# Moving a two-layer decoder kernel's operands by 96 bytes, reading its position bias reversed, and spreading the down products over the last quad

## The chip, the cores and the metric

The kernel runs on one core of a Trainium2 chip, as one program in one launch. The metric is device time in microseconds (us). Before the change three runs took 2271.83, 2272.42 and 2274.74 us, so the median is 2272.42 us. Smaller is better.

## The reference

Two layers of a decoder trunk work on 512 positions of 1024 channels, in float32. Each layer is

```
x = x + 0.5 * SwiGLU(RMSNorm(x))          # FFN 1, hidden width 2816
h = RMSNorm(x);  z = h @ w_in             # one combined projection
p_A = conv module, p_B = short gated conv
p_C = sliding-window attention (window 128, shared T5 relative bias)
p_D = forgetting attention
x = x + (sum_i sigmoid(gate_i) * p_i) @ w_out
x = x + 0.5 * SwiGLU(RMSNorm(x))          # FFN 2
```

The relative bias that p_C adds to its scores depends only on the distance between query and key. For one head it is a band matrix: row p is one fixed line of 384 numbers, shifted by p places. The kernel builds that matrix once, as the tile `bias` (128 partitions, 4 heads, 256 keys), and uses it in both layers.

## The kernel before, in words

**Arithmetic.** Every large product is done as three matmuls in the type float32r: each operand is split into a high part and a rest, and `mm3` sums high x high, high x rest and rest x high. The stationary operand is 128x128, and each matmul loads its own. Moving operands are 512 columns wide in the projections and the down products (`X` and `hs` tiles, and `L` tiles in the mixer), and 256 wide in most of the FFN (`th` high, `tl` rest).

**Weights.** They stream from HBM in chunks of 512 KB over the SyncE (SP) queue into the tiles `ws` and `X`. ScalarE (ACT) then casts a chunk to its high part `h` (line 292) and VectorE (DVE) subtracts to get the rest `l` (line 299). `nextw` keeps a few chunks ahead of TensorE (PE).

**The FFN.** There are 22 hidden tiles. The first four are plain products against `X` (`proj`, `proj2`). Beside them DVE and ACT prepare `th` and `tl` from x, a quarter in each call of `halves`. The other 18 go in nine pairs, one per call of `quad`, by a Strassen scheme: seven products of 24 matmuls each, named by their moving operand (B11, B21, T2, T3, T1, B22, T4). In a call, `begin` issues the next pair's B11 between T1 and B22, and the last product, T4, has a chain behind it: DVE subtracts, ACT takes the Silu, DVE multiplies, ACT and DVE split the result into two `hs` tiles. The hidden tiles are cut into three segments (`SEGS`). After each segment `down` multiplies its `hs` tiles by the down weights: two groups `mg` of four 128-row outputs, and in each a loop over chunks `kc`, where chunk kc uses the hs tiles of pair kc of that segment.

**Setup.** `setup` is a generator that starts in the first FFN of the first layer and is carried on at `tick`. It makes the line of 384 numbers for each head (a matmul at line 599, an add at line 601), writes it to a scratch tensor `toep` in DRAM 128 times, row after row with a pitch of 385 (line 604), and reads `toep` back with a pitch of 384, so that row p comes out shifted by p (line 606). Both transfers are issued by GpSimd (POOL). TensorE takes no part in it beyond line 599.

**Where tiles lie.** Tiles come from pools that are laid out one behind the other in SBUF. Pool `odd` (small tiles) comes first, then `sb` (weights, x, X), then the pools of a stage. So the sum of the small tiles sets where everything behind them starts. In the program before, the weight tiles and the tiles X, L, hs, `pth` and `ptl` start 96 bytes past a multiple of 128 bytes. `th` and `tl` start 32 bytes past one, since a tile `off` of 64 bytes is put ahead of them. PSUM has two groups of four banks, `mm` and `bg`.

**Order.** The program's order on each engine is fixed when it is built: a scheduler places instructions by their dependences, so it may pull some of a later product's matmuls into a place where an engine would wait.

Of the kernel before, what the change touches and what calls it, by code (L numbers as in the profile page):

```python
# [32 lines left out]
P = 128  # L33
# [4 lines left out]
FF = 2816  # L38
NF = 22
SEGS = ((0, 8), (8, 16), (16, 22))  # L40
NSTD = 4

B11, B21, B22, T1, T3, T2, T4 = range(0, 1792, 256)
# [21 lines left out]
C_1 = 640  # L65
C_OH = 641
C_NEG = C_OH + 384
NCST = C_NEG + 384

SWA_PAIRS = ((0, 2), (1, 3))  # L70
NMM = 4
# [8 lines left out]
def _trunk(tc, xin, wst, wa, wv, wf, par, relb, cst, out):  # L80
    nc = tc.nc
    ctx = ExitStack()

    odd = ctx.enter_context(tc.tile_pool(name="odd", bufs=1))
    sb = ctx.enter_context(tc.tile_pool(name="sb", bufs=1))
    psp = ctx.enter_context(tc.tile_pool(name="ps", bufs=1, space=bass.MemoryType.PSUM))
    uid = [0]
# [17 lines left out]
    def PSM():  # L105
        uid[0] += 1
        return psp.tile([P, S], F32, tag="mm", bufs=NMM, name=f"mm_{uid[0]}")
# [84 lines left out]
    def item(kind, n, srcs, q=False, raw=RW, a1=None, turn=0):  # L192
        items.append((kind, n, srcs, raw, q, a1 or (4 if q else 2), 3 if q else 2, turn))

    def chunk(kind="w", k=1, **kw):
        nonlocal ci
        item(kind, 1024, [wst[ci + i] for i in range(k)], **kw)
        ci += k

    def ffn_items():  # L200
        for _ in range(2 * NSTD):
            chunk()
        f0, nq, q = len(items), (NF - NSTD) // 2, 0
        both = RW + RX
        chunk("A11", q=True)
        for t0, t1 in SEGS:
            for t in range(max(t0, NSTD), t1, 2):
                kw = dict(q=True, raw=both, turn=f0)
                if q:
                    chunk("A12", **kw)  # L210
                else:
                    chunk("A12", q=True)
                chunk("S2", 2, a1=None if q else 2, **kw)
                item("S3", 1024, [], **kw)
                item("S1", 1024, [], **kw)
                q += 1
                if q < nq:
                    chunk("A11", **kw)
                item("S4", 1024, [], **kw)
                item("A22", 1024, [], **kw)  # L220
            for _ in range(2 * ((t1 - t0) // 2)):
                if t1 < NF:
                    chunk(**kw)
                else:
                    chunk()
# [215 lines left out]
    def down(hs, mg, nk, after):  # L441

        pss = [PSM() for _ in range(4)]
        for kc in range(nk):
            w = kt(nextw(), S)
            for c in range(4):
                for kk in range(2):
                    mm3(pss[c], (w[0][:, kk, c * P:(c + 1) * P], w[1][:, kk, c * P:(c + 1) * P]),
                        hs[2 * kc + kk], kc == 0 and kk == 0, kc == nk - 1 and kk == 1)
                if kc == nk - 1:  # L450
                    after(4 * mg + c, pss[c])

    def ffn(st, nxt, fin=None, first=False):
        cx = open_stage("ffn", "tf")
# [56 lines left out]
            V.tensor_mul(us, us, sg)  # L511
            put(us)

        def quad(t):

            a, c11 = nxtq[0] or begin()
            w, b = nextw(), PSM()
            product(b, w, B21, True)
            V.tensor_add(c11, c11, b)
            w = nextw()  # L520
            product(a, w, T2)
            cc = T([P, 2 * S], F32, "cc", 2, pool="ffn").rearrange("p (s h c) -> p s h c", s=2, h=2)
            A.copy(cc[:, :, 0, :], gu(a))
            w, c = nextw(), PSM()
            product(c, w, T3, True)
            w = nextw()
            product(a, w, T1)
            A.copy(cc[:, :, 1, :], gu(a))
            V.tensor_sub(cc[:, :, 1, :], gu(c), cc[:, :, 1, :])
            nxtq[0] = begin() if t + 2 < NF else None  # L530
            w = nextw()
            product(a, w, B22)
            sg = TP()
            A.activation(sg[:, 0:256], c11[:, 0:256], AF.Silu)
            A.activation(sg[:, 256:S], a[:, 0:256], AF.Silu)
            V.tensor_mul(sg[:, 0:256], sg[:, 0:256], c11[:, 256:S])
            V.tensor_mul(sg[:, 256:S], sg[:, 256:S], a[:, 256:S])
            put(sg)
            w = nextw()
            product(c, w, T4)  # L540
            V.tensor_sub(cc[:, :, 0, :], gu(c), cc[:, :, 0, :])
            sg = TP()
            A.activation(sg, cc[:, 0].rearrange("p h c -> p (h c)"), AF.Silu)
            V.tensor_mul(sg, sg, cc[:, 1].rearrange("p h c -> p (h c)"))
            put(sg)

        for t0, t1 in SEGS:
            hs.clear()
            for t in range(t0, min(NSTD, t1)):
                wg, wu = kt(nextw()), kt(nextw())  # L550
                pg, pu = PSM(), PSM()
                if t < 1:
                    proj2(st, wg, pg, wu, pu)
                else:
                    halves(t)
                    proj(st, wg, pg)
                    proj(st, wu, pu)
                if first and t == 0:
                    spawn(setup())
                if t == 0:  # L560
                    halves(0)
                hidden(pg, pu, st.rb)
                tick()
            for t in range(max(NSTD, t0), t1, 2):
                quad(t)
                tick()
            last = t1 == NF

            def after(d, ps):
                stt(x[d], ps, 0.5, x[d], ALU.mult, ALU.add)  # L570
                if last and nxt is not None:
                    norm_split(nxt, d)
                if last and fin is not None:
                    fin(d)

            for mg in range(2):
                down(hs, mg, (t1 - t0) // 2, after)
            if last and nxt is not None:
                spawn(norm_end(nxt))
        cx.close()  # L580
# [6 lines left out]
    def setup():  # L587
        V.tensor_copy(idb, ident)
        V.tensor_copy(cmb, ct[:, C_CM:C_CM + P])
        rt = T([32, 4], F32, "rt")  # L590
        nc.gpsimd.dma_start(rt, relb)
        oh = TP()
        nc.gpsimd.dma_start(oh[0:32, 0:384], cst[0:32, C_OH:C_OH + 384])
        ng = TP()
        nc.gpsimd.dma_start(ng[0:4, 0:384], cst[0:4, C_NEG:C_NEG + 384])
        yield
        yield
        ps = PSB()
        mm(ps[0:4, 0:384], lhsT=rt, rhs=oh[0:32, 0:384], start=True, stop=True)
        br = TP()  # L600
        V.tensor_add(br[0:4, 0:384], ps[0:4, 0:384], ng[0:4, 0:384])
        scr = tc.dram_tile([4, P * 385], F32, name="toep")
        dst = bass.AP(tensor=scr.tensor, offset=scr.offset, ap=[[P * 385, 4], [385, P], [1, 384]])
        nc.gpsimd.dma_start(dst, br[0:4, 0:384].rearrange("p (o c) -> p o c", o=1).to_broadcast([4, P, 384]))
        src = bass.AP(tensor=scr.tensor, offset=scr.offset + 127, ap=[[384, P], [P * 385, 4], [1, 256]])
        nc.gpsimd.dma_start(bias, src)


    def mixer(l, st, nxt):
        cx = open_stage("mix", "modd")  # L610


        cacc = [None, None]
# [108 lines left out]
        def fox_unit(h, i):  # L722
# [14 lines left out]
                A.activation(p[:, 0:W], p[:, 0:W], AF.Identity, scale=sm)  # L737
                yield
                if i == 0:
                    ptile["h"] = T([P, 2048], F32R, "pth", pool="mix").rearrange("p (q j c) -> p q j c", q=4, j=4)  # L740
                    ptile["l"] = T([P, 2048], F32R, "ptl", pool="mix").rearrange("p (q j c) -> p q j c", q=4, j=4)
                    V.memset(f(ptile["h"][:, 2, 3, :]), 0.0)
                    V.memset(f(ptile["l"][:, 2, 3, :]), 0.0)
                pT = PSB()
# [28 lines left out]
        def swa_unit(pr, n):  # L773
# [23 lines left out]
                yield  # L797
                yield
                if n == 0:
                    stile["h"] = T([P, 2048], F32R, "pth", pool="mix").rearrange("p (h s c) -> p h s c", h=2, s=8)  # L800
                    stile["l"] = T([P, 2048], F32R, "ptl", pool="mix").rearrange("p (h s c) -> p h s c", h=2, s=8)
                    V.memset(f(stile["h"][:, :, 6, :]), 0.0)
                    V.memset(f(stile["l"][:, :, 6, :]), 0.0)
                pT = PSB()
# [189 lines left out]
            norm_split(nxt, d)  # L994

        for mg in range(2):
            down(mT, mg, 4, after)
        spawn(norm_end(nxt))
        cx.close()

# [30 lines left out]
def _constants():  # L1031
    c = np.zeros((P, NCST), np.float32)
    p = np.arange(P)
    c[:, C_ONE:C_ONE + P] = 1.0 / D
    c[:, C_ID:C_ID + P] = np.eye(P)
    c[:, C_TRI:C_TRI + P] = p[:, None] <= p[None]
    c[:, C_TRI + P:C_TRI + 2 * P] = 1.0
    c[:, C_CM:C_CM + P] = np.where(p[None] <= p[:, None], 0.0, NEG)
    c[:, C_1] = 1.0
    b = _buckets()  # L1040
    for e in range(384):
        dist = 255 - e
        if 0 <= dist < P:
            c[b[dist], C_OH + e] = 1.0
        else:
            c[:, C_NEG + e] = NEG
    return c
# [100 lines left out]
```

## Time and profile before

| what | value |
|---|---|
| median of three runs | 2272.42 us |
| the profiled execution's own time | 2276.64 us |
| its span (first to last instruction) | 2274.9 us |
| mean granted TensorE clock | 0.99 |
| PE busy | 2234.0 us, 98% of the span, 13059 matmuls |
| PE weight loads busy | 1973.6 us, 87% |
| DVE busy | 1542.3 us, 68% |
| ACT busy | 1004.0 us, 44% |
| POOL busy | 3.8 us |
| DMA | 217.81 MB, mean 96 GB/s |

The profile is of one execution. A busy PE means that some matmul is in its pipeline; it does not say how fast matmuls follow each other, which is read from their start times. The profile also gives the granted clock: 1.0 is the level of 2.4 GHz and 0.5 is that of 1.2 GHz. The profile divides the span into 40 slices of 57 us; the clock stands at 9 tenths or more in all of them but the second, where it stands at 6.

### The profile page before, as it was taken

The page shows a single profiled execution, that of the slowest core. Times are in us where ns is not written, and L with a number is a line of the kernel's source. Part 1 is how long each engine was busy: PE and PEld are TensorE (multiplying, and loading weights), DVE is VectorE, ACT ScalarE, POOL GpSimd, SP SyncE. Part 2 cuts the span into 40 slices and gives each one's busy share as a digit, 9 for nine tenths or more (in the row PEclk, how much of TensorE's full clock was granted, in tenths as well). Part 3 has the DMA queues.
Part 4 walks back from the last instruction along what each step waited for, and adds up shares of the span by engine and source line. Part 5 has one row for each costly group of instructions (what it writes and reads, how often), then busy time and mean ns, then how long its engine had stood idle before and what let it go on. Part 6 is the DMA issues. An engine that isn't in the chain of part 4 may idle for free.

```text
span 2274.9 us, 31903 instructions
## 1 busy us (share of the span) xinstructions
PE 2234.0 (98%) x13059; PEld 1973.6 (87%) x13059; DVE 1542.3 (68%) x2234; ACT 1004.0 (44%) x1506; POOL 3.8 (0%) x9
## 2 busy tenths in 40 slices
PE   9599999999999999999999999999999999999999
PEld 6589998988888889898989898988888888899998
DVE  7658576776665487575688585676767645957664
ACT  4335343465433355352455252454544333534432
POOL 0000000000000000000000000000000000000000
PEclk9699999999999999999999999999999999999999
DMA  5433312322223334232124232223222222432312
GB/s 147 126 112 95 119 47 84 93 81 78 75 74 100 105 95 149 90 111 94 59 90 158 95 100 93 70 86 96 75 80 69 92 93 93 130 130 85 129 47 84
DMA packets 62146, 217.81 MB, mean 96 GB/s; under 512 B 7408, under 2 KB 7540, under 8 KB 62000
## 3 DMA queue, kind: packets, MB, share of 16 engines
q1 hardware_dynamic: 61056, 214.41, 29.0%
q0 software_dynamic: 944, 1.37, 0.4%
q8 instruction: 102, 1.67, 0.3%
q14 instruction: 44, 0.36, 0.1%
HBM read 212.87 MB, written 2.88 MB: 95 GB/s over the span
## 4 chain that ended last, share of the span: by engine, by line
PE 95%; DMA 2%; DVE 1%; ACT 1%; issue 0%; SPq 0%; ACTq 0%; DVEq 0%
PE mm L347 20%; PE mm L349 20%; PE mm L348 20%; PE bg L483 6%; PE bg L486 6%; PE bg L485 6%; PE mm L483 4%; PE mm L486 4%; PE mm L485 4%; DMA ws<-wst 1%; DMA X<-wst 1%; PE bg L746 0%; PE bg L906 0%; PE bg L730 0%; PE bg L371 0%
## 5 line engine op out<-in xcount | busy, mean ns | idle before, releaser
L299 DVE TENSOR_TENSOR l<-ws,h 128x1024 fp32r<-128x1024 f32 (+2 forms) x246 | 295.9, 1204 | 345.8 <-ACT h L292 276.6
L292 ACT CAST h<-X 128x1024 fp32r<-128x1024 f32 x264 | 277.3, 1053 | 442.3 <-PE mm L348 193.1
L299 DVE TENSOR_TENSOR l<-X,h 128x1024 fp32r<-128x1024 f32 x264 | 320.7, 1221 | 186.0 <-PE mm L349 74.3
L292 ACT CAST h<-ws 128x1024 fp32r<-128x1024 f32 (+2 forms) x246 | 255.0, 1038 | 429.8 <-PE mm L348 256.3
L347 PE MATMUL mm<-X,h 128*128 128x512 f32 x928 | 364.2, 395 | 0.6 <-ACT h L352 0.5
L349 PE MATMUL mm<-X,l 128*128 128x512 f32 x928 | 363.0, 391 | 0.0
L348 PE MATMUL mm<-X,h 128*128 128x512 f32 x928 | 361.8, 391 | 0.7 <-DVE X L159 0.6
L483 PE MATMUL bg<-th,h 128*128 128x256 f32 x1152 | 327.1, 284 | 30.9 <-ACT h L292 22.2
L486 PE MATMUL bg<-th,l 128*128 128x256 f32 x1152 | 325.4, 283 | 0.6 <-DVE l L299 0.6
L485 PE MATMUL bg<-tl,h 128*128 128x256 f32 x1152 | 325.2, 282 | 0.0
L347 PE MATMUL mm<-hs,h 128*128 128x512 f32 x704 | 274.1, 389 | 0.0
L349 PE MATMUL mm<-hs,l 128*128 128x512 f32 x704 | 273.9, 389 | 0.0
L348 PE MATMUL mm<-hs,h 128*128 128x512 f32 x704 | 273.9, 389 | 0.0
L483 PEld LDWEIGHTS bg<-th,h 128*128 128x128 f32 x1152 | 219.9, 191 | 33.9 <-ACT h L292 24.1
L483 PE MATMUL mm<-th,h 128*128 128x256 f32 x864 | 243.5, 282 | 3.3 <-ACT h L292 3.3
L485 PE MATMUL mm<-tl,h 128*128 128x256 f32 x864 | 242.2, 280 | 0.0
L486 PE MATMUL mm<-th,l 128*128 128x256 f32 x864 | 242.1, 280 | 0.0
L486 PEld LDWEIGHTS bg<-th,l 128*128 128x128 f32 x1152 | 220.1, 191 | 1.4 <-DVE l L299 1.4
L485 PEld LDWEIGHTS bg<-tl,h 128*128 128x128 f32 x1152 | 219.3, 190 | 0.1
L349 PEld LDWEIGHTS mm<-X,l 128*128 128x128 f32 x928 | 174.2, 188 | 39.4 <-DVE l L299 2.9
L347 PEld LDWEIGHTS mm<-X,h 128*128 128x128 f32 x928 | 174.2, 188 | 38.3 <-ACT h L352 1.6
L348 PEld LDWEIGHTS mm<-X,h 128*128 128x128 f32 x928 | 174.4, 188 | 37.6 <-DVE X L159 1.5
(231 smaller groups left out, 3491.3 us busy)
## 6 DMA issues: line engine op xcount, KB each, us to landing
ws<-wst SPq DMA_DIRECT2D x234, 512.0 KB, 3.3
X<-wst SPq DMA_DIRECT2D x144, 512.0 KB, 3.4
ws<-wf SPq DMA_DIRECT2D x8, 512.0 KB, 3.4
ws<-wv SPq DMA_DIRECT2D x8, 388.0 KB, 3.0
ws<-wa SPq DMA_DIRECT2D x8, 384.0 KB, 3.1
x<-xin SPq DMA_DIRECT2D x8, 256.0 KB, 6.2
out<-x SPq DMA_DIRECT2D x8, 256.0 KB, 2.0
ws<-wst SPq DMA_DIRECT2D x4, 256.0 KB, 6.0
```

The lines of the kernel that those rows point to most:

```text
L292: A.copy(hi, src)
L299: V.tensor_sub(lo, src, f(hi))
L347: mm(ps, lhsT=w[0], rhs=xx[0], start=first, stop=False)
L348: mm(ps, lhsT=w[0], rhs=xx[1], start=False, stop=False)
L349: unit[0] = mm(ps, lhsT=w[1], rhs=xx[0], start=False, stop=last)
L483: mm(d, lhsT=w[0][:, c], rhs=t0, start=first and s == 0 and k == 0, stop=False, skip_group_check=True)
L485: mm(d, lhsT=w[0][:, c], rhs=t1, start=False, stop=False, skip_group_check=True)
L486: mm(d, lhsT=w[1][:, c], rhs=t0, start=False, stop=s == 1 and k == 3, skip_group_check=True)
```

## The change

Three edits stand in the diff.

The first puts a tile `pad` of 96 bytes at the head of pool `odd`. With the new small tile `turn` (512 bytes) everything behind them starts 608 bytes later. The weight tiles and X, L and hs now start 64 bytes past a multiple of 128, and `th` and `tl` start on one. `pth` and `ptl` move to a pool of their own, `mpt`, behind a tile of 64 bytes, and start on a multiple of 128 too. The constants in `cst` (the identity for transposes among them) go from a multiple of 128 to 96 past one.

The second changes how `bias` is built. The line of 384 numbers is written once per head (6 KB in all). It is read back so that partition p starts at element p of the line, which gives the rows in reverse order. A 128x128 matrix `turn`, ones on the other diagonal, is loaded from the constants, and two matmuls of 512 columns with it turn the partitions over; ACT copies each result back over `bias`.

The third makes `down` a generator that yields after each chunk. The last call of `quad` in each FFN gets the first group's `down` as `fill`: chunk kc=0 runs where `begin` stood, between T1 and B22, and chunk kc=1 runs between B22 and T4. The chunks' order in the weight stream follows.

```diff
@@ -82,6 +84,7 @@
     odd = ctx.enter_context(tc.tile_pool(name="odd", bufs=1))
+    odd.tile([P, PAD], F32, tag="pad", name="pad")
@@ -216,9 +219,13 @@
                 if q < nq:
                     chunk("A11", **kw)
+                else:
+                    chunk(**kw)
                 item("S4", 1024, [], **kw)
+                if q == nq:
+                    chunk(**kw)
                 item("A22", 1024, [], **kw)
-            for _ in range(2 * ((t1 - t0) // 2)):
+            for _ in range(t1 - t0 if t1 < NF else t1 - t0 - 2):
@@ -449,6 +456,7 @@
                 if kc == nk - 1:
                     after(4 * mg + c, pss[c])
+            yield
@@ -521,13 +530,13 @@
-            w, c = nextw(), PSM()
+            w, c = nextw(), PSB() if fill else PSM()
             product(c, w, T3, True)
...
-            nxtq[0] = begin() if t + 2 < NF else None
+            nxtq[0] = next(fill) if fill else begin()
             w = nextw()
             product(a, w, B22)
...
             put(sg)
+            if fill:
+                next(fill)
             w = nextw()
             product(c, w, T4)
...
-            for mg in range(2):
-                down(hs, mg, (t1 - t0) // 2, after)
+            dn = [down(hs, mg, (t1 - t0) // 2, after) for mg in range(2)]
+            for t in range(max(NSTD, t0), t1, 2):
+                quad(t, dn[0] if t + 2 == NF else None)
+                tick()
+            for g in dn:
+                for _ in g:
+                    pass
@@ -599,15 +612,23 @@
-        scr = tc.dram_tile([4, P * 385], F32, name="toep")
-        dst = bass.AP(tensor=scr.tensor, offset=scr.offset, ap=[[P * 385, 4], [385, P], [1, 384]])
-        nc.gpsimd.dma_start(dst, br[0:4, 0:384].rearrange("p (o c) -> p o c", o=1).to_broadcast([4, P, 384]))
-        src = bass.AP(tensor=scr.tensor, offset=scr.offset + 127, ap=[[384, P], [P * 385, 4], [1, 256]])
-        nc.gpsimd.dma_start(bias, src)
+        scr = tc.dram_tile([4, 384], F32, name="toep")
+        nc.gpsimd.dma_start(scr, br[0:4, 0:384])
+        nc.gpsimd.dma_start(bias, bass.AP(tensor=scr.tensor, offset=scr.offset, ap=[[1, P], [384, 4], [1, 256]]))
+        turn_ = T([P, P], F32, "turn")
+        nc.gpsimd.dma_start(turn_, cst[:, C_J:C_J + P])
+        for _ in range(3):
+            yield
+        for i in range(2):
+            ps, b = PSB(), bias[:, 2 * i:2 * i + 2, :].rearrange("p h c -> p (h c)")
+            mm(ps, lhsT=turn_, rhs=b, start=True, stop=True)
+            A.copy(b, ps)
     def mixer(l, st, nxt):
-        cx = open_stage("mix", "modd")
+        cx = open_stage("mix", "mpt", "modd")
+        T([P, 16], F32, "off", pool="mpt")
```

The first place at which the order changes is in the first call of `quad` on TensorE. The names are the output bank, the moving operand and the weight tile; `h` is a weight's high part and `l` its rest. In the program before, after the first pair's B11 (bank bg_607) and B21 (mm_640), two matmuls of a later B11 (bg_770) are pulled forward, and T2 follows at once:

```order
L485 MATMUL mm_640<-tl_50_185,h_100_425 128x256
L486 MATMUL mm_640<-th_46_181,l_506 128x256
L483 MATMUL bg_770<-th_43_178,h_134_634 128x256
L485 MATMUL bg_770<-tl_47_182,h_134_634 128x256
L483 MATMUL bg_607<-th_43_178,h_593 128x256
L485 MATMUL bg_607<-tl_47_182,h_593 128x256
```

In the changed program the two matmuls with `turn` stand at that place:

```order
L491 MATMUL bg_773<-th_43_179,h_135_637 128x256
L493 MATMUL bg_773<-tl_47_183,h_135_637 128x256
L625 MATMUL bg_875<-bias_78,turn_408 128x512
L625 MATMUL bg_878<-bias_78,turn_408 128x512
L491 MATMUL bg_610<-th_43_179,h_596 128x256
L493 MATMUL bg_610<-tl_47_183,h_596 128x256
```

What moved: nothing of the pair's own order, but TensorE now comes to two instructions that need the tile `bias` from DRAM after about 50 matmuls of the first pair.

The second place is the last call of `quad` in the first FFN, on TensorE, behind T4. In the program before, T4 (bank mm_3111) is followed by the rest of chunk kc=0 and then by kc=1, with hs tiles that were ready long ago:

```order
L483 MATMUL mm_3111<-th_46_181,h_3079 128x256
L485 MATMUL mm_3111<-tl_50_185,h_3079 128x256
L486 MATMUL mm_3111<-th_46_181,l_3109 128x256
L348 MATMUL mm_3239<-hs_421_2809,h_3164 128x512
L349 MATMUL mm_3239<-hs_420_2808,l_3166 128x512
L347 MATMUL mm_3240<-hs_415_2772,h_3164 128x512
L348 MATMUL mm_3240<-hs_416_2773,h_3164 128x512
```

In the changed program T4 (bank bg_3126) is followed by chunk kc=2, the last one. Twelve matmuls use the hs tiles of the product B22 (hs_475 and hs_476), three for each of four banks, and then come those that use the two that T4 itself yields (hs_484, then hs_485):

```order
L493 MATMUL bg_3126<-tl_50_186,h_467_3151 128x256
L494 MATMUL bg_3126<-th_46_182,l_473_3185 128x256
L354 MATMUL mm_3181<-hs_475_3240,h_3246 128x512
L355 MATMUL mm_3181<-hs_476_3241,h_3246 128x512
L356 MATMUL mm_3181<-hs_475_3240,l_3248 128x512
...
L356 MATMUL mm_3184<-hs_475_3240,l_3248 128x512
L354 MATMUL mm_3181<-hs_484_3308,h_3246 128x512
L354 MATMUL mm_3182<-hs_484_3308,h_3246 128x512
L354 MATMUL mm_3183<-hs_484_3308,h_3246 128x512
L354 MATMUL mm_3184<-hs_484_3308,h_3246 128x512
L355 MATMUL mm_3181<-hs_485_3309,h_3246 128x512
```

What moved: of the 48 matmuls of chunks kc=0 and kc=1, 44 stood behind T4 (the scheduler had put four ahead of B22) and all stand ahead of it now. Between T4 and the first matmul that needs its result there are 12 matmuls where there were 47.

## Rows read from the trace of the kernel before

**Rows 1.** The page's busy time per engine: us, share of the span, instructions.

```profile
PE 2234.0 (98%) x13059; PEld 1973.6 (87%) x13059; DVE 1542.3 (68%) x2234; ACT 1004.0 (44%) x1506; POOL 3.8 (0%) x9
```

**Rows 2.** Stretches of the span: from:to and length in us, busy us.

```profile
core 0: us, PE busy (x) PEld busy (x) DVE busy (x) ACT busy (x) POOL busy (x), PEclk, DMA share, GB/s
54.84:110.00 55.16, 29.09 (x180) 27.44 (x179) 34.37 (x43) 20.08 (x28) 0.78 (x1) 0.69 0.42 116
...
57.30:84.60 27.30, 8.60 (x37) 8.01 (x38) 11.79 (x20) 6.65 (x10) 0.78 (x1) 0.50 0.47 125
```

**Rows 3.** Same view: first pairs of layer 2's first FFN; middle of an FFN.

```profile
1205.60:1235.00 29.40, 26.83 (x221) 26.01 (x221) 27.73 (x31) 18.44 (x25) 0.00 (x0) 1.00 0.37 127
...
300.00:345.00 45.00, 45.00 (x385) 45.00 (x384) 37.11 (x41) 25.30 (x34) 0.00 (x0) 1.00 0.15 48
```

**Rows 4.** Waits from 45 to 97 us: waiter, releaser; total us, times, longest.

```profile
POOL bias L606 <- DMA toep<-tp: 35.3, 1, 35.3
ACT h L292 <- DMA ws<-wst: 23.7, 2, 18.3
...
PE bg L483 <- ACT h L292: 16.5, 2, 11.7
...
PE bg L483 <- ACT th L352: 8.6, 1, 8.6
```

**Rows 5.** POOL in order of time: start us, us, what [idle before, releaser].

```profile
42.41 1.15 POOL L604 DMA_DIRECT2D toep<-tp  x1 [24.88 <-DVE tp L601]
78.89 0.78 POOL L606 DMA_DIRECT2D bias<-toep  x1 [35.32 <-DMA toep<-tp]
```

**Rows 6.** DMA issues: what, queue, count, KB each, median us to landing.

```profile
X<-wst SPq DMA_DIRECT2D x144, 512.0 KB, 3.4
...
toep<-tp POOLq DMA_DIRECT2D x1, 768.0 KB, 36.2
bias<-toep POOLq DMA_DIRECT2D x1, 512.0 KB, 6.2
...
tp<-cst POOLq DMA_DIRECT2D x1, 6.0 KB, 1.8
```

**Rows 7.** The chain of waits: start us, us, what (line 599, two passes).

```profile
32.49 0.73 PE bg L599 x2
```

**Rows 8.** PE in order of time, the projection ahead of the first pair.

```profile
52.12 0.39 PE L349 MATMUL mm<-X,l 128*128 128x512 f32 x1
...
54.84 0.39 PE L349 MATMUL mm<-X,l 128*128 128x512 f32 x1
```

**Rows 9.** The same, one product of 24 in a pair and the next's first.

```profile
300.59 0.28 PE L483 MATMUL bg<-th,h 128*128 128x256 f32 x1
...
303.42 0.28 PE L483 MATMUL mm<-th,h 128*128 128x256 f32 x1
```

**Rows 10.** The same, sliding-window attention's products with pth and ptl.

```profile
501.64 0.28 PE L826 MATMUL bg<-pth,vh 128*128 128x256 f32 x1
...
502.72 0.28 PE L826 MATMUL bg<-pth,vh 128*128 128x256 f32 x1
```

**Rows 11.** PE's groups by line and shape: count, busy us, mean ns, idle before.

```profile
L347 PE MATMUL mm<-X,h 128*128 128x512 f32 x928 | 364.2, 395 | 0.6 <-ACT h L352 0.5
...
L483 PE MATMUL bg<-th,h 128*128 128x256 f32 x1152 | 327.1, 284 | 30.9 <-ACT h L292 22.2 <-ACT th L352 8.6
...
L347 PE MATMUL mm<-hs,h 128*128 128x512 f32 x704 | 274.1, 389 | 0.0
...
L483 PE MATMUL mm<-th,h 128*128 128x256 f32 x864 | 243.5, 282 | 3.3 <-ACT h L292 3.3
...
L347 PE MATMUL mm<-L,h 128*128 128x512 f32 x256 | 99.6, 389 | 0.0
L347 PE MATMUL mm<-h,X 128*128 128x512 f32 x64 | 25.9, 404 | 0.0
```

**Rows 12.** PE behind T4 of the first FFN's last pair.

```profile
355.24 0.39 PE L348 MATMUL mm<-hs,h 128*128 128x512 f32 x1
```

**Rows 13.** ACT and DVE there: split of T4's result.

```profile
358.68 0.62 ACT L352 CAST hs<-tp 128x512 fp32r<-128x512 f32 x1 [1.36 <-DVE su L922]
...
359.33 0.69 DVE L353 TENSOR_TENSOR hs<-tp,hs 128x512 fp32r<-128x512 f32 x1 [0.64 <-ACT hs L352]
```

More of the change, by code (lines that the diff above doesn't have):

```diff
@@ L40 @@
 SEGS = ((0, 8), (8, 16), (16, 22))
+PAD = 24
 NSTD = 4
@@ L67 @@
 C_NEG = C_OH + 384
-NCST = C_NEG + 384
+C_J = C_NEG + 384
+NCST = C_J + P
 SWA_PAIRS = ((0, 2), (1, 3))
@@ L512, in hidden, with quad @@
             put(us)
-        def quad(t):
+        def quad(t, fill=None):
             a, c11 = nxtq[0] or begin()
@@ L563, in ffn @@
                 tick()
-            for t in range(max(NSTD, t0), t1, 2):
-                quad(t)
-                tick()
             last = t1 == NF
@@ L739, in fox_unit @@
                 if i == 0:
-                    ptile["h"] = T([P, 2048], F32R, "pth", pool="mix").rearrange("p (q j c) -> p q j c", q=4, j=4)
-                    ptile["l"] = T([P, 2048], F32R, "ptl", pool="mix").rearrange("p (q j c) -> p q j c", q=4, j=4)
+                    ptile["h"] = T([P, 2048], F32R, "pth", pool="mpt").rearrange("p (q j c) -> p q j c", q=4, j=4)
+                    ptile["l"] = T([P, 2048], F32R, "ptl", pool="mpt").rearrange("p (q j c) -> p q j c", q=4, j=4)
                     V.memset(f(ptile["h"][:, 2, 3, :]), 0.0)
@@ L799, in swa_unit @@
                 if n == 0:
-                    stile["h"] = T([P, 2048], F32R, "pth", pool="mix").rearrange("p (h s c) -> p h s c", h=2, s=8)
-                    stile["l"] = T([P, 2048], F32R, "ptl", pool="mix").rearrange("p (h s c) -> p h s c", h=2, s=8)
+                    stile["h"] = T([P, 2048], F32R, "pth", pool="mpt").rearrange("p (h s c) -> p h s c", h=2, s=8)
+                    stile["l"] = T([P, 2048], F32R, "ptl", pool="mpt").rearrange("p (h s c) -> p h s c", h=2, s=8)
                     V.memset(f(stile["h"][:, :, 6, :]), 0.0)
@@ L996, in mixer @@
         for mg in range(2):
-            down(mT, mg, 4, after)
+            for _ in down(mT, mg, 4, after):
+                pass
         spawn(norm_end(nxt))
@@ L1039, in _constants @@
     c[:, C_1] = 1.0
+    c[p, C_J + P - 1 - p] = 1.0
     b = _buckets()
```

## The prediction

> **What bounds the kernel now.** I read the page's busy times first. TensorE (PE) is busy for 2234.0 us of 2274.9 [rows 1], and no other engine comes near, so time goes down only where PE has less to do, waits less, or is fed faster. Three readings follow: where PE waits, at what clock it runs there, and how closely matmuls follow each other elsewhere.
>
> The waits stand in one place, between 45 and 97 us, at the first FFN's first pairs. PE waits 16.5 us in two pieces (the longer 11.7) for ACT's cast of a weight chunk and 8.6 us for another cast. ACT waits 23.7 us, of which 18.3 at once, for that chunk's DMA `ws` [rows 4]. Such a chunk lands in 3.4 us in the median [rows 6]. The waits have a neighbour: POOL issues the write to `toep` at 42.41 us and can issue the read of `bias` only at 78.89 [rows 5]. That write takes 36.2 us for 768 KB [rows 6], about 21 GB/s, and the late `ws` falls into its time. I read the write as the cause of the late chunk.
>
> The wait has a second price. Behind it the granted clock is 0.50, the 1.2 GHz level, from 57.3 to 84.6 us [rows 2]. Before it fell PE had been idle since its last projection matmul at 54.84 [rows 8].
>
> Away from there PE is packed, so pitch is read from start times. In a projection 12 pitches take 54.84 - 52.12 = 2.72 us: 226.7 ns for 512 columns [rows 8]. In a pair 24 take 2.83 us: 117.9 ns for 256 columns [rows 9]. At 2.4 GHz 512 columns last 213.3 ns and 256 last 106.7. The surplus is 13.4 and 11.2 ns. With `pth` the same 256 columns take 1.08 us / 9 = 120.0 ns [rows 10], a surplus of 13.3. Operands that start 96 bytes past a multiple of 128 thus pay 32 columns' time; `th`, 32 bytes past one, pays about 26.
>
> **The write to toep.** From 54.84 to 110 us PE issues 180 matmuls of the pairs in 55.16 us [rows 2]. At 117.9 ns they need 21.2, so 34.0 us are lost to waits and half clock together. The same place in layer 2, with no such write beside it, issues 221 in 29.40 us [rows 3], which need 26.1: 3.3 us are lost there, to preparing `th` (DVE is busy 27.73 of the 29.40 us). If the write is short, the first FFN should look like that one: 34.0 - 3.3 = 30.7 us saved. The new write is 6 KB, and a 6 KB transfer on the same queue took 1.8 us [rows 6].
>
> The new matrix `turn` costs POOL one issue, for which nothing on PE waits early. PE gets two fp32 matmuls of 512 columns. Line 599's, of 384 columns and two passes, held it for 0.73 us [rows 7]; two of 512 come to 2 x 0.73 x 512/384 = 1.95, say 2.0 us. ACT's two copies lie beside PE.
>
> These two matmuls add a wait as well: they stand in PE's order, and everything of the first pair is queued behind them. PE gets there 50 matmuls after 54.84 us, at 54.84 + 50 x 0.118 = 60.7. `bias` should land at 42.41 + 1.15 + 1.8 (write) + 0.8 + 6.2 (read, as long as before [rows 5, 6]) = 52.4. The cover is 8 us, so I cost the wait at nothing. Each us beyond it is lost, and the clock may fall again.
>
> **Down chunks between products.** Before, B22 already had four pulled-forward matmuls ahead of it, so the new filler removes no wait that the list shows: 0 saved. Behind T4 something is lost. PE goes on at 355.24 us [rows 12]; the chain behind T4 gives the high part at 358.68 + 0.62 = 359.30 and the rest at 359.33 + 0.69 = 360.02 [rows 13], 4.06 and 4.78 us later. Before, 47 matmuls (10.7 us) covered that. Now 12 do: 12 x 0.2267 = 2.72 us, so PE waits 1.34 us. Four more take 0.91, by which time the rest is there. In four FFNs: 5.4 us. The lower end is 0: without a weight split in their way DVE's and ACT's four operations, each of 0.6 to 0.7 us, would just fit under the cover. I take 5.4.
>
> **The 96 bytes.** Float32r matmuls of 512 columns are 3 x (928 + 704 + 256 + 64) = 5,856, of 256 columns with `th` or `tl` 3 x (1152 + 864) = 6,048 [rows 11]; together 11,904. The trace holds no matmul at the new places, so I bound the effect. Upper end: the whole surplus goes, 5,856 x 13.4 + 6,048 x 11.2 = 146 us. Below nothing: if starting nearer to a multiple of 128 were to cost what being farther from it now seems to, 8 columns (3.33 ns) a matmul, 40 us are lost. Between them: both kinds move 32 bytes nearer to the multiple of 128 below them, and 32 bytes are 8 columns, 3.33 ns at 2.4 GHz. The one step the trace shows, `pth` to `th`, moves 64 bytes for 120.0 - 117.9 = 2.1 ns, the same sign and a smaller slope, and 0 is near it. The other reading, that a matmul pays for whole lines of 128 bytes, fits 226.7 (17 x 13.33) and 120.0 (9 x 13.33) but not 117.9; by it the 512-wide keep 17 lines and `th` falls from 9 to 8, which at the 106.7 ns of its columns is at most 11.2 x 6,048 = 68 us. By the step's slope 32 bytes are 1.05 ns, 12.5 us in all; by lines up to 68. I take the 8 columns, 3.33 x 11,904 = 39.7 us, which lie midway between. If PE gains that in the pairs, DVE is still not the bound: 37.11 us in 45.00 [rows 3] become 37.11 in about 43.7. The identity for transposes goes to a worse place; at 8 columns for some 250 matmuls that is under 1 us.
>
> Two statements of the Trainium skill speak to this, one against. SBUF — State Buffer, Door 1: The DMA port swizzle, says that accesses go by lines of 16 bytes. Every start before and after is a multiple of 16, so by that rule the move changes nothing and the sum is the first rival's; that 13.3 and 11.2 ns differ between two such starts speaks against it, but weakly. TensorE: Matmul & The Clock Gate, Back-to-back issue gap, gives N/2.4 + 2.5 ns, 215.8 and 109.2 here: the rows' 226.7 and 117.9 lie above it, and by it a matmul freed of the surplus would save 10.9 and 8.7 ns, 116 us in all, an estimate that lands in the second rival.
>
> **Sum.** Against the profiled execution's 2276.6 us: - 30.7 + 2.0 + 5.4 - 39.7 = - 63.0, so 2213.6. The median of the runs shown is 4.2 us under that execution, so 2209.
>
> **Rivals.** First, the place of operands doesn't matter. For it: every matmul here brings a new stationary operand, and the surplus may be the price of that change, wherever it lies. Against it: 13.3 and 11.2 ns at equal width. Time: 2209 + 39.7 = 2249.
>
> Second, most of the surplus goes: two thirds of 146 is 97 us, so 2209 - (97 - 40) = 2152. For it: at 13 ns the surplus is large; against it: only a step of 2.1 ns is seen.
>
> Third, the late chunk has another cause than the write, and the stall stays: 2209 + 30.7 = 2240. Against it: the coincidence in time, and that layer 2's first FFN, built alike, has no such wait [rows 3].
>
> Fourth, slower than before: the new places are worse. Place: each of the 11,904 matmuls. It decides from (30.7 - 7.4) / 11,904 = 1.96 ns a matmul on; at 8 columns, 3.33 ns, the time is 2249 + 40 = 2289. For it: the 512-wide operands don't come to a multiple of 128, and the weights move as well, so what serves one may hurt the other. Against it: the step seen has the other sign.
>
> A late `bias` is a smaller matter: landing 10 us after 60.7 costs about 10 us plus half clock behind it, some 20 us, and leaves the kernel faster in all cases but the fourth.
>
> **How the numbers follow.** Forecast (placement gives 1 to 6 ns a matmul) 0.45; first rival 0.27; second 0.18; third 0.06; fourth 0.04. The likeliest gives 2209, and its own range is 2177 to 2237. The range takes in the first and third rivals with some us for a late `bias` or a clock that stays low longer, 2256, and most of the second's cases, 2135. A difference under 0.2% (4.5 us) can't be told from none in this kernel. Slower by more than that holds in the fourth case, 0.04; within it, in what lies between that case and the first, 0.02; faster, 0.94.
>
> **What would show it.** Write: a `toep` transfer near 2 us, no ACT wait for `ws` over 5 us before 100 us, clock 1.0 from 55 to 95. If that stretch still shows the wait, the first term fails. Turn: two fp32 matmuls of about 1 us each near 60 us, with no DMA named as their releaser. Tail: a PE wait of 1 to 1.5 us for an `hs` tile of ACT behind T4, four times. Placement: start times in the same views, 223 and 114.5 ns in place of 226.7 and 117.9. If these stay at 226.7 and 117.9 the first rival holds; at 216 and 109 the second; above, the fourth.

## The result and the profile after

The changed kernel takes 2253.17 us (median of 4 runs, 2252.79 to 2253.62) against 2272.25 of the kernel before in the same session: ratio 0.9914 [0.9897, 0.9931], 19.1 us less. The forecast was 2209. The profiled execution took 2253.28 us, with a span of 2251.5.

The page's busy times, answering [rows 1]:

```profile
PE 2230.1 (99%) x13063; PEld 1968.4 (87%) x13063; DVE 1542.8 (69%) x2234; ACT 1005.0 (45%) x1508; POOL 3.8 (0%) x10
```

PE still bounds the kernel and is busy for only 3.9 us less. So what was gained is mostly waiting, and matmuls can't have become cheaper by much.

The stretches of [rows 2]:

```profile
core 0: us, PE busy (x) PEld busy (x) DVE busy (x) ACT busy (x) POOL busy (x), PEclk, DMA share, GB/s
54.84:110.00 55.16, 48.19 (x373) 45.99 (x372) 46.45 (x57) 30.84 (x43) 0.00 (x0) 0.97 0.40 133
57.30:84.60 27.30, 21.43 (x153) 19.75 (x154) 26.32 (x34) 15.86 (x23) 0.00 (x0) 0.94 0.40 134
```

373 matmuls now fit where 180 did: 360 of the pairs, 9 of 512 columns, and the 4 passes of the two turn matmuls. At 117.9 and 226.7 ns the first two kinds need 44.5 us, the turn takes 1.9 (below), and 55.16 - 46.4 = 8.8 us are lost, where 34.0 were. The granted clock is 0.94 in place of 0.50. The second row shows something else: VectorE (DVE) is now busy for 26.32 us of 27.30.

The waits there, from 30 to 97 us, as in [rows 4] (waiter, releaser; total us, times, longest):

```profile
PE bg L491 <- ACT h L299: 4.7, 1, 4.7
...
ACT h L299 <- DMA ws<-wst: 3.2, 1, 3.2
...
PE bg L491 <- ACT th L359: 1.8, 1, 1.8
POOL bias L618 <- DMA toep<-tp: 1.4, 1, 1.4
```

PE's 16.5 and 8.6 us have become 4.7 and 1.8; ACT's 23.7 for `ws` are 3.2. GpSimd (POOL) in order of time and the issues of its queue answer [rows 5, 6]:

```profile
42.31 0.52 POOL L616 DMA_DIRECT2D toep<-tp  x1 [24.88 <-DVE tp L614]
44.26 0.82 POOL L618 DMA_DIRECT2D bias<-toep  x1 [1.43 <-DMA toep<-tp]
```

```profile
bias<-toep POOLq DMA_DIRECT2D x1, 512.0 KB, 7.7
turn<-cst POOLq DMA_DIRECT2D x1, 64.0 KB, 5.0
toep<-tp POOLq DMA_DIRECT2D x1, 6.0 KB, 1.7
```

The write lands in 1.7 us and `bias` at 44.26 + 7.7 = 52.0. TensorE in order of time: the turn matmuls, then a projection and a pair to set against [rows 8, 9], and attention's product against [rows 10].

```profile
52.03 0.39 PE L356 MATMUL mm<-X,l 128*128 128x512 f32 x1
...
54.75 0.39 PE L356 MATMUL mm<-X,l 128*128 128x512 f32 x1
...
63.15 1.88 PE L625 MATMUL bg<-bias,turn 128*128 128x512 f32 x4
69.77 0.39 PE L491 MATMUL bg<-th,h 128*128 128x256 f32 x1 [4.75 <-ACT h L299]
...
300.10 0.28 PE L491 MATMUL mm<-th,h 128*128 128x256 f32 x1
...
302.93 0.28 PE L491 MATMUL bg<-th,h 128*128 128x256 f32 x1
...
478.76 0.28 PE L847 MATMUL bg<-pth,vh 128*128 128x256 f32 x1
...
479.82 0.28 PE L847 MATMUL bg<-pth,vh 128*128 128x256 f32 x1
```

12 pitches in 2.72 us are 226.7 ns and 24 in 2.83 us 117.9, both as before. Only `pth` moved: 9 pitches in 1.06 us, 117.8 ns where there were 120.0. The turn names no releaser and holds PE for 1.88 us, so `bias` was there.

Behind T4 of the first FFN's last pair, TensorE:

```profile
342.15 0.40 PE L354 MATMUL mm<-hs,h 128*128 128x512 f32 x1
...
344.68 0.39 PE L356 MATMUL mm<-hs,l 128*128 128x512 f32 x1
345.14 0.96 PE L354 MATMUL mm<-hs,h 128*128 128x512 f32 x3
```

ACT and DVE there, to set against [rows 13]:

```profile
344.46 0.62 ACT L359 CAST hs<-tp 128x512 fp32r<-128x512 f32 x1 [0.76 <-DVE tp L555]
...
345.12 0.69 DVE L360 TENSOR_TENSOR hs<-tp,hs 128x512 fp32r<-128x512 f32 x1 [0.69 <-ACT hs L359]
```

Twelve down matmuls run from 342.15. The thirteenth was due at 344.68 + 0.23 = 344.91 and starts at 345.14, behind ACT's cast, which ends at 344.46 + 0.62 = 345.08. So 0.23 us are lost there, and 0.57 us in all up to the end of this FFN, with two more pitches some 0.11 too long; by the same start times 0.49, 0.51 and 0.41 in the other three. For four FFNs that is about 2 us.

### The profile page after: what moved, and what is told of

It reads as the page before. It is cut to its first block, busy times and chain, and to the rows that moved or that the text cites. A ratio compares the mean times of both kernels' runs of the same rounds, so it can differ in the third digit from the quotient of the medians.

```text
span 2251.5 us, 31919 instructions
## 1 busy us (share of the span) xinstructions
PE 2230.1 (99%) x13063; PEld 1968.4 (87%) x13063; DVE 1542.8 (69%) x2234; ACT 1005.0 (45%) x1508; POOL 3.8 (0%) x10
## 4 chain that ended last, share of the span: by engine, by line
PE 96%; DVE 1%; DMA 1%; ACT 1%; issue 0%; SPq 0%; ACTq 0%; DVEq 0%
PE mm L354 20%; PE mm L356 20%; PE mm L355 20%; PE bg L491 6%; PE bg L494 6%; PE bg L493 6%; PE mm L491 4%; PE mm L494 4%; PE mm L493 4%; DMA X<-wst 1%; PE bg L767 0%; PE bg L927 0%; PE bg L751 0%; DMA ws<-wst 0%; PE bg L378 0%
## 5 line engine op out<-in xcount | busy, mean ns | idle before, releaser
L306 DVE TENSOR_TENSOR l<-X,h 128x1024 fp32r<-128x1024 f32 x272 | 330.7, 1221 | 197.5 <-PE bg L494 74.4
L491 PE MATMUL bg<-th,h 128*128 128x256 f32 x1216 | 343.1, 282 | 10.7 <-ACT h L299 8.9
L493 PE MATMUL bg<-tl,h 128*128 128x256 f32 x1216 | 341.8, 281 | 0.0
L494 PE MATMUL bg<-th,l 128*128 128x256 f32 x1216 | 341.3, 281 | 0.0
L491 PEld LDWEIGHTS bg<-th,h 128*128 128x128 f32 x1216 | 230.6, 190 | 13.0 <-ACT h L299 10.6
L494 PEld LDWEIGHTS bg<-th,l 128*128 128x128 f32 x1216 | 230.6, 190 | 0.2 <-DVE l L306 0.2
L493 PEld LDWEIGHTS bg<-tl,h 128*128 128x128 f32 x1216 | 229.9, 189 | 0.6 <-DVE tl L360 0.2
L491 PE MATMUL mm<-th,h 128*128 128x256 f32 x800 | 224.8, 281 | 3.7 <-ACT h L299 3.7
L493 PE MATMUL mm<-tl,h 128*128 128x256 f32 x800 | 223.6, 279 | 0.0
L494 PE MATMUL mm<-th,l 128*128 128x256 f32 x800 | 223.4, 279 | 0.0
```

Of the source, the lines that this page charges most:

```text
L306: V.tensor_sub(lo, src, f(hi))
L491: mm(d, lhsT=w[0][:, c], rhs=t0, start=first and s == 0 and k == 0, stop=False, skip_group_check=True)
L493: mm(d, lhsT=w[0][:, c], rhs=t1, start=False, stop=False, skip_group_check=True)
L494: mm(d, lhsT=w[1][:, c], rhs=t0, start=False, stop=s == 1 and k == 3, skip_group_check=True)
```

## The experiments

Fifteen kernels ran. Where a kernel was timed four times or more, a ratio to the kernel before stands with its 95% interval; the others ran once. Each trace is of one execution. In the expectations, a "distance" is the moving operand's start in SBUF minus the stationary operand's, modulo 128 or 256 bytes. `h`, `l` (and `vh`, `vl`) are the stationary operands, `X`, `hs`, `th` (and `pth`) the moving ones.

**The parts, one by one.** The kernel before with the new bias build alone:

```diff
-        scr = tc.dram_tile([4, P * 385], F32, name="toep")
...
+        scr = tc.dram_tile([4, 384], F32, name="toep")
+        nc.gpsimd.dma_start(scr, br[0:4, 0:384])
...
+            mm(ps, lhsT=turn_, rhs=b, start=True, stop=True)
+            A.copy(b, ps)
```

> The kernel before with one edit: the position bias is written once per head, read reversed and turned over by two matmuls. No pad, old order of the down products. Theory W (all of the gain comes from the short write): the changed kernel lost about 10 us between 54.84 and 110 us where the kernel before lost 34.0, so 24 us less than the profiled 2276.6, or 19 to 20 us less than the median: 2252 to 2254 us, with the granted clock at 1.0 or close to it from 57 to 70 us. Theory M (the three edits share the gain): 2258 us or more.

2253.27 us, 0.9917 [0.9902, 0.9932]. Its waits from 45 to 97 us and the stretch of [rows 2]:

```profile
PE bg L484 <- ACT h L293: 4.8, 1, 4.8
...
ACT h L293 <- DMA ws<-wst: 3.0, 1, 3.0
```

```profile
54.84:110.00 55.16, 48.77 (x369) 46.67 (x368) 45.19 (x56) 29.93 (x42) 0.00 (x0) 0.94 0.38 129
```

Nearly the same waits, the same number of matmuls but four, and the same time as the whole change: this edit alone carries the gain. The reverse, the changed kernel with the old build (the same lines with + and - exchanged):

> The changed kernel with the position bias built the old way (768 KB written to DRAM by four partitions). Theory W: the stall of the first pairs comes back, ACT waits over 15 us for a weight chunk, the granted clock is 0.5 for over 20 us, and the time is 2272 to 2277 us. Theory M: 2266 us or less.

2275.86 us, 1.0009 [0.9999, 1.0018]. Its waits from 45 to 97 us:

```profile
POOL bias L619 <- DMA toep<-tp: 34.0, 1, 34.0
ACT h L299 <- DMA ws<-wst: 22.6, 2, 17.2
...
PE bg L491 <- ACT h L299: 15.6, 2, 10.7
...
PE bg L491 <- ACT th L359: 8.5, 1, 8.5
```

With the long write the late chunk is back, and the gain is gone. So the old build makes the chunk late, and by the times of [rows 4, 5] it is its write, since the read comes later. What in the write does it no run separates. The other two parts together are worth nothing, or a few us of loss.

The kernel before with the 96 bytes alone:

```diff
+    odd.tile([P, 24], F32, tag="pad", name="pad")
```

> The kernel before with one edit: a tile of 96 bytes ahead of everything in pool odd, so that th and tl start on a multiple of 128 bytes and the other operands 64 past one. Theory W: no change, 2268 to 2277 us, pitches of 226.7 and 117.8 ns as before. Theory M: at least 6 us less, 2266 us or lower, and a pitch below 226 or 117 ns. The prediction's term for this edit was 39.7 us: 2232 us.

2272.54 us, 0.9998 [0.9988, 1.0007]. TensorE in a down product (36 pitches) and in a pair (24):

```profile
355.44 0.39 PE L350 MATMUL mm<-hs,l 128*128 128x512 f32 x1
...
363.60 0.39 PE L350 MATMUL mm<-hs,l 128*128 128x512 f32 x1
```

```profile
300.26 0.28 PE L484 MATMUL bg<-th,h 128*128 128x256 f32 x1
...
303.09 0.28 PE L484 MATMUL mm<-th,h 128*128 128x256 f32 x1
```

8.16 / 36 = 226.7 ns and 2.83 / 24 = 117.9: the move of all operands by 96 bytes changes nothing.

The changed kernel with the down products in their old order:

```diff
...
-            nxtq[0] = next(fill) if fill else begin()
+            nxtq[0] = begin() if t + 2 < NF else None
...
-            if fill:
-                next(fill)
...
-                quad(t, dn[0] if t + 2 == NF else None)
+                quad(t)
```

> The changed kernel with the down products back behind T4 of the last pair. In the changed kernel's trace PE loses about 0.5 us behind T4 in each of three FFNs read, 2 us in four. Theory W: 2 us less than the changed kernel's 2253.2, about 2251, and no PE wait behind T4. Rival (the chunks between the products hide a wait that the list of waits doesn't show): 2256 us or more.

2249.98 us, 0.9903 [0.9886, 0.9919]. Its trace loses 0.02 us behind T4 of the first FFN, where the changed kernel's loses 0.57. The chunks between the products cost 2 us by the traces and 3 by the medians (2253.17 - 2249.98; the two intervals overlap). They take no wait away. A single difference of 3 us between kernels is not safe here: the bias build alone (2253.27) also has the old order, and differs from this kernel only by the 96 bytes and the place of `pth` and `ptl`.

**Why the first FFN still loses 8.8 us.** One account is that the bias read, 512 KB beside the weight chunks, holds them up; the other that DVE is the bound there. The changed kernel with the bias build spawned after the third pair:

```diff
-                if first and t == 0:
-                    spawn(setup())
...
+                if first and t == 8:
+                    spawn(setup())
```

> The changed kernel with the whole setup of the position bias begun after the third pair of the first FFN in place of beside the first tile, so that no bias transfer and neither of the two matmuls falls between 40 and 75 us. Theory D (the changed kernel's rest of a stall there, some 10 us with the half clock, comes from the bias read of 512 KB beside the weight chunk, which lands in 6.6 us and not in 3.4): the loss from 54.84 to 110 us falls to the 3.3 us of layer 2's first FFN, 5 to 7 us less, about 2247 us. Rival (DVE is the bound there: it prepares th and cannot catch up): the wait of 4.7 us stays and the time stays within 2 us of 2253, less the 2 us of the moved matmuls only if these were on the path.

2251.26 us, 0.9905 [0.9888, 0.9922]. Three of its waits from 45 to 97 us, and the stretch from 40 to 75 us:

```profile
PE bg L491 <- ACT h L299: 5.2, 1, 5.2
...
ACT h L299 <- DVE X L286: 2.3, 1, 2.3
...
ACT h L299 <- DMA ws<-wst: 0.3, 1, 0.3
```

```profile
40.00:75.00 35.00, 29.50 (x173) 26.36 (x172) 34.26 (x48) 18.04 (x26) 0.00 (x0) 0.90 0.43 151
```

Of the wait for `ws` 0.3 us are left, and PE waits as long as before for the cast, with DVE busy for 34.26 us of 35.00. The end of that wait, on DVE, ACT and TensorE in turn:

```profile
62.87 1.22 DVE L286 TENSOR_TENSOR X<-X,ws 128x1024 f32<-128x1024 f32 x1
64.12 3.13 ACT L299 CAST h<-X 128x1024 fp32r<-128x1024 f32 x3 [2.25 <-DVE X L286]
65.22 0.58 PE L491 MATMUL bg<-th,h 128*128 128x256 f32 x1 [5.16 <-ACT h L299]
```

The cast starts when DVE has its sum of two weight chunks ready (line 286), and DVE works without a gap from 60.52 us on. In the changed kernel's trace the cast at 68.67 us waits 2.88 us for the same line. So the bias read is not the cause: DVE, which also prepares `th` and the low parts of the weights, holds that place. No run took work off DVE, so what that would return is not known. This with the old down order, 2250.21 us, 0.9904 [0.9887, 0.992], is the base of the later runs:

> The changed kernel with the old order of the down products and the setup of the position bias begun after the third pair: the two single gains joined. If they add: 3 us and 2 us under 2253, about 2248, with 226.7 and 117.8 ns as pitches. If the late setup gave nothing (2251.26 against 2253.17 lay within the runs' scatter): about 2250.

The gains of the two edits don't add up to anything that shows.

**What the pitch hangs on, if not on the place.** `th` and `pth` differ in their distance to the stationary operand, and the edit moved both operands alike, except for `pth`, whose distance went from 0 to 64 bytes, and whose pitch is the one that changed. So I moved the moving operands against the weights, in the changed kernel, by 64, 32 and 96 bytes (the first is shown; the others have 8 and 24 in the gap's place and for `th`, and 24 and 8 for `ofw`):

```diff
+    wp = ctx.enter_context(tc.tile_pool(name="wp", bufs=1))
+    gp = ctx.enter_context(tc.tile_pool(name="gp", bufs=1))
+    gp.tile([P, 16], F32, tag="gap", name="gap")
...
-        pool = stage[pool] if pool else odd if n % 2048 else sb
+        pool = stage[pool] if pool else odd if n % 2048 else wp if tag in ("h", "l") else sb
...
-            return T([P, 1024], dt, n, pool="ffn")
+            return T([P, 1024], dt, n, pool="ffw")
...
-        cx = open_stage("ffn", "tf")
+        cx = open_stage("ffn", "ffw", "tf")
+        T([P, 16], F32, "ofw", pool="ffw")
```

The tiles in `ffw`, which pairs and most down products use beside those in `wp`, lie 128 bytes farther modulo 256. So in these three kernels the distances hold modulo 128 only.

> The changed kernel with all moving operands of the large products (X, hs, L, th, tl) starting 64 bytes past the stationary ones (h, l) modulo 128, where X, hs and L start at the same place as h and l now; th and tl keep their distance of 64. Theory R (what counts is the distance between the moving and the stationary operand, not where either starts: distance 0 costs 32 columns over the width, 64 costs 26): the pitch of 512 columns falls from 226.7 to 224.2 ns, 2.5 ns x 5,856 = 14.6 us less, about 2239 us. Theory N (the place of operands doesn't matter for 512 columns): 226.7 ns and 2253 us.

> The same with a distance of 32 bytes for X, hs, L, th and tl. Theory R: pitch of 512 columns between 224 and 227 ns, and th's of 256 columns at or above 117.8 and at or below 120.0; a distance that is no multiple of 64 could also cost more than 0 does. Theory N: 226.7 and 117.8, as in the changed kernel.

> The same with a distance of 96 bytes. Theory R, if the pattern is even about 64: the pitches of the distance of 32. If it falls with distance all the way: 512 columns below 224 ns, 256 below 117.6. Theory N: 226.7 and 117.8.

At 64 bytes 2244.41 us, 0.9872 [0.9857, 0.9887]; at 32 and 96 bytes 2289.95 and 2291.93, one execution each. TensorE at 64 bytes, in a pair (24 pitches) and in two stretches of down products (36 each):

```profile
299.82 0.28 PE L498 MATMUL bg<-th,l 128*128 128x256 f32 x1
...
302.54 0.28 PE L498 MATMUL bg<-th,l 128*128 128x256 f32 x1
...
345.62 0.39 PE L359 MATMUL mm<-hs,l 128*128 128x512 f32 x1
...
353.95 0.39 PE L359 MATMUL mm<-hs,l 128*128 128x512 f32 x1
...
357.38 0.39 PE L359 MATMUL mm<-hs,l 128*128 128x512 f32 x1
...
365.62 0.39 PE L359 MATMUL mm<-X,l 128*128 128x512 f32 x1
```

And at 32 bytes, 36 pitches:

```profile
350.42 0.39 PE L358 MATMUL mm<-hs,h 128*128 128x512 f32 x1
...
358.82 0.39 PE L358 MATMUL mm<-hs,h 128*128 128x512 f32 x1
```

The 512-wide matmuls come at 231.4 (with one gap of 307) and 228.9 ns at 64 bytes and at 233.3 at 32 (at 96 the mean is 233.4): worse than the 226.7 of distance 0 everywhere, so the expectation of 224 fell. But in the pairs 24 pitches take 2.72 us, 113.3 ns, at 64 bytes. By the start times of all matmuls the means are 113.7 for `th` and `tl` and 230.1 for the 512-wide: 229.4 with `X` and 229.1 with `L`, whose weight tiles all lie at 64 modulo 256, and 231.2 with `hs`. 6,048 x (117.8 - 113.7) = 24.8 us gained and 5,856 x (230.1 - 227.4) = 15.8 lost make 9.0; the medians differ by 2253.2 - 2244.4 = 8.8. That is also the lowest median of the study.

The distance of `th` is 64 bytes in the changed kernel too, and there its pitch is 117.8. Two theories: the distance counts modulo 256 (Q), or at one and the same distance the timing of the stream picks one of two rhythms (T). `th` at 192 bytes in place of 64, on the base:

```diff
-        T([P, 16], F32, "off", pool="tf")
+        T([P, 48], F32, "off", pool="tf")
```

> The kernel of the two joined gains with th and tl 128 bytes farther on, 192 bytes past the weight tiles modulo 256 in place of 64; all other operands as they are. In the run with a distance of 64 for all operands th followed at 113.3 ns in nearly all of the run, with part of its weight tiles at a distance of 192, and in one stretch of the late-setup run at 114 ns with a distance of 64. Theory Q (the distance modulo 256 decides): 113.3 ns, 4.45 ns x 6,048 = 27 us less, 2221 us. Theory T (how the matmuls fall in time decides, and any distance of 64 modulo 128 can show either): 117.8 ns in most stretches or a mixture, 2221 to 2248 us.

2245.97 us (2241.35 to 2247.35), 0.9878 [0.9864, 0.9893]. 27% of these matmuls come at 113.3 ns and the others at 117.8, in stretches, at the same addresses: against Q. With `th` there and the 512-wide at 128 bytes, and with `th` at 64 and these at 192 (gap tiles of 32 and 48 elements, as in the diff above):

> The same with X, hs and L 128 bytes past the weight tiles modulo 256, and th 192. Theory P128 (only the distance modulo 128 counts): 226.7 ns for 512 columns, as at distance 0. Theory Q: another pitch, above or below.

> The same with X, hs and L 192 bytes past the weight tiles modulo 256, and th 64. Theory P128: about 229.7 ns for 512 columns, as in the run with a distance of 64, and 117.8 or 113.3 for th. Theory Q: another pitch for 512 columns.

One execution each: 2260.1 us, with the 512-wide at a mean of 232.8 ns and 92% of `th` at the quick rhythm; 2281.49, at 233.2 and with 9%. Distance 0 stays the best for 512 columns.

T was then put to a test that moves no operand: one more matmul of 32 or 96 columns ahead of each pair's first product, whose output is overwritten.

```diff
+            mm(a[:, 0:32], lhsT=w[0][:, 0:P], rhs=th[0][:, B11:B11 + 32], start=True, stop=True,
+               skip_group_check=True)
             product(a, w, B11, True)
```

> The kernel of the two joined gains (th 64 bytes past the weights, 117.8 ns throughout) with one more matmul of 32 columns ahead of each pair's product B11, 36 in all, whose result is overwritten by that product. Theory T (two rhythms are possible at the same places, and how the matmuls fall in time picks one): at least one stretch of 50 us in which th follows at 113.3 to 115 ns. Theory Q (place alone decides): 117.8 ns in all stretches, and the time is 1 to 4 us longer than 2250.

> The same with 96 columns in the extra matmul. Theory T: again some stretches at 113.3 to 115 ns, not the same ones. Theory Q: 117.8 throughout.

> The kernel with th and tl 192 bytes past the weights modulo 256, which showed 113.3 ns in some stretches and 117.8 in others at the same places, with the extra matmul of 32 columns ahead of each pair's B11. Theory T: the share of stretches at 113.3 changes; if every pair starts in the quicker rhythm, up to 18 us less than 2246. Theory Q: stretches as without it, 2246 to 2250 us.

On the base 2254.88 and 2253.6 us, one execution each; on the kernel with `th` at 192 bytes 2246.56, 0.9883 [0.9862, 0.9904]. TensorE near 828 us on the base, 24 pitches:

```profile
827.21 0.28 PE L487 MATMUL bg<-th,h 128*128 128x256 f32 x1
...
830.04 0.28 PE L487 MATMUL mm<-th,h 128*128 128x256 f32 x1
```

The same product with 32 columns ahead of the pair:

```profile
828.18 0.28 PE L487 MATMUL bg<-th,h 128*128 128x256 f32 x1
...
830.90 0.28 PE L487 MATMUL mm<-th,h 128*128 128x256 f32 x1
```

2.83 us become 2.72, 117.9 ns become 113.3, with every operand where it was. On the kernel with 192 bytes other stretches changed, some up and some down, and the share of the quick rhythm went from 27 to 29%. So the address does not pick the rhythm alone. On the base the quick rhythm holds for 37 us with 32 columns (from 828 us) and for some 26 us with 96, in the same place: 7 and 4% of these matmuls. Theory T had named 50 us, and other places for the second. The changed kernel with the late setup shows 113.3 ns too, from 74 to 104 us, with no short matmul and no operand moved. With one trace of each kernel it is not shown that the short matmuls made the difference, and not chance between executions. What picks the rhythm is open, and none of these matmuls paid for itself.

## Why the prediction was wrong

**The 96 bytes: the step that failed.** "I take the 8 columns, 3.33 x 11,904 = 39.7 us": measured, 0.9998 [0.9988, 1.0007], nothing. Even by the step that I had, 32 bytes were 1.05 ns; the 3.33 were a choice midway between two readings, and no row showed them. I read the 2.1 ns between `pth` and `th` as the price of an absolute place. The two also differ in their distance to the stationary operand, and that I had not written down; the edit shifts both operands and leaves it. The row was read rightly, the variable was not: `pth` alone changed its distance, and gained the 2.2 ns. The Trainium skill, SBUF — State Buffer, Door 1: The DMA port swizzle, which goes by lines of 16 bytes, read as in the prediction gave the right answer for a shift of both operands, with this ratio to bear it out; it does not give the 226.7, 230 and 233 ns that the distances bring. The formula in the Trainium skill, TensorE: Matmul & The Clock Gate, Back-to-back issue gap, which the page gives for single isolated matmuls, was reached by no run: 113.3 against its 109.2 and 226.7 against its 215.8 are the lowest pitches that I read.

**The write: right mechanism, too large.** It was to return 30.7 us; by the stretch's rows it returned 34.0 - 8.8 = 25.2, and its edit with the turn 2273.18 - 2253.27 = 19.9 in medians, against 30.7 - 2.0 = 28.7. I took layer 2's first FFN, with 3.3 us lost, for the model. Here PE still waits 4.7 and 1.8 us, with DVE busy for 26.32 of 27.30. But DVE was nearly as busy in the model (27.73 of 29.40 us), so why 8.8 us are lost here and 3.3 there stays open. The test "no ACT wait for `ws` over 5 us" passed (3.2); "clock 1.0 from 55 to 95" did not (0.94 up to 84.6). I had also measured against a profiled execution 4.2 us over the median, and how much of its 34.0 us was of that kind I could not see from one execution: the old build in the changed kernel loses less in the same stretch (192 matmuls against 180).

**The turn: right.** 2.0 us forecast, 1.88 measured, no DMA as releaser; `bias` forecast at 52.4, landed at 52.0, with PE there at 63.15 and not 60.7.

**The tail: right sign, too large.** 5.4 us forecast, about 2 in the trace. I took the high part at 4.06 us after T4, as in [rows 12, 13], where ACT waits 1.36 us for DVE. Here it is there at 345.08 - 342.15 = 2.93 us, just behind a cover of 2.76, and PE waits 0.23 us, not the 1 to 1.5 that I had named as the sign. That is near the lower end I had named, for the case that no weight split stands in the way.

**The sum.** From the profiled 2276.6: - 25.2 + 1.9 + 2 + 0 = 2255.3, against 2253.3 measured; 2 us stay unassigned. The first rival, "the place of operands doesn't matter", at 2249 and 0.27, is what happened: of the 44 us between 2209 and 2253 the placement term alone is 39.7. Its reason, that the surplus is paid "wherever it lies", was still not the whole truth, since a different distance changes the surplus.

## What to carry to other kernels

Where two rows differ, list all that differs between them before you name the variable, and ask whether the edit changes that one: here both operands moved together, and their distance stayed. When a stall goes, look which engine is busiest in that stretch, since it may set what remains: DVE at 26.32 of 27.30 us, hidden before behind a late DMA. And a DMA that TensorE does not wait for can stop it through another queue's weight chunks: here 768 KB from 4 partitions, 36.2 us long, with a wait of up to 18.3 us for a chunk.

## What the runs showed that I had not expected

The pitch of float32r matmuls at full clock changes with the distance between the moving and the stationary operand. For 512 columns: 226.7 ns at 0 bytes, a mean of 230.1 at 64, 233.3 at 32, and means of 233.4 at 96, 232.8 at 128 and 233.2 at 192 (0 and 128 modulo 256 are not the same; 32, 64 and 96 hold modulo 128, as said above). For 256 columns: 120.0 at 0 (`pth`), means of 118.5 at 32 and 119.2 at 96, and at 64 and 192 either 117.8 or 113.3. Which of these two comes changes over one execution at fixed addresses. It was the quick one for over 90% of the matmuls in two kernels whose 512-wide operands lay at 64 or 128 bytes, but for 9% where they lay at 192. What decides it was not settled. For 512 columns each distance but 0 was read at one absolute place, and in one trace.

Two kernels have lower medians than both that this study began with, and their executions overlap: the 64-byte distance for all moving operands (2244.41 us, 0.9872 [0.9857, 0.9887]) and `th` at 192 bytes (2245.97, 0.9878 [0.9864, 0.9893]).
